# A hybrid attention / delta-net layer on one core: the arena moved to a multiple of 1,024 bytes, weight tiles and constant matrices moved directly behind it

## The chip, the cores and the metric

The kernel runs on one core of a Trainium2 chip. A core has five engines that run on their own and wait for each other through semaphores: TensorE (PE, matrix multiplies, with a separate weight load, PEld, before each), VectorE (DVE), ScalarE (ACT), GpSimd (POOL) and SyncE (SP), whose queue issues all the loads and stores here. Operands lie in the on-chip memory SBUF, as 128 partitions; a tile is a stretch of bytes at the same offset in each partition. TensorE's results go to PSUM, here one tensor "banks" of eight banks of 512 float32 columns.

The metric is the time of one execution on the device in microseconds (us), the median of several. Lower is better.

## The reference

One layer over 512 latent tokens and 256 context tokens, width 1,024, everything in float32. Cut to what matters:

```python
h  = rms_norm(x, g_norm1) * (1.0 + sc1) + sh1
hc = rms_norm(ctx, g_norm1) * (1.0 + csc1) + csh1
aq, ak, av, dq, dk, dv, dz, da, db, ga, gd = split_cols(h @ w_in)        # the same of hc
y_attn = window_ctx_attention(q_a, k_a, v_a, k_ac, v_ac, attn_sink)
o_dc, s_cf, s_cb = bidir_delta(*dn_inputs(cdq, cdk, cdv, cda, cdb), s_zero, s_zero)
o_dl, _, _ = bidir_delta(*dn_inputs(dq, dk, dv, da, db), s_cf, s_cb)
y = jax.nn.sigmoid(ga) * (y_attn @ w_br_attn) + jax.nn.sigmoid(gd) * (y_d @ w_br_dn)
x_new = x + gt1 * (y @ w_out)
hm = rms_norm(x_new, g_norm2) * (1.0 + sc2) + sh2
out = x_new + gt2 * (jnp.square(jax.nn.relu(hm @ w_mlp1)) @ w_mlp2)       # hidden width 4,096
```

`y_d` is the delta-net output, normalised and gated with `silu(dz)`. The shifts, scales and gates `sh, sc, gt` come from `silu(c) @ w_ada + b_ada`.

## The kernel before, in words

**Layout of the work.** Activations are kept transposed: 128 features by tokens, so that a weight tile of 128 x 128 is TensorE's weight operand and the activations stream past it, 512 or 256 columns (tokens) in one matmul. Each float32 operand is split in two parts, a rounded one (hi) and the rest (lo), and each product of two tiles is made of three matmuls into the same bank: hi by hi, hi by lo, lo by hi. That is `mm3` with L299 (`w[0]`, `xhi`), L300 (`w[0]`, `xlo`) and L301 (`w[1]`, `xhi`); L978 (gate tiles), L1024 (attention branch) and L1427 (`Pair.prod`) write out the same three.

**Where things lie in SBUF.** Two kinds of memory hold nearly all operands:

- The **arena** is one tensor of 167 units of 1,024 bytes per partition, allocated first (L107 and L108). `mem` hands out stretches of whole units; the tensors called `m` in the profile are such stretches. Activations, their hi and lo parts, and in some places weights lie there.
- **Pools** behind it: `const` holds constants (`ones`, `ident`, `bones`, `identb`, `maskb`, `prm` and small per-token tables), `sb` holds the rotating **weight tiles** of 4,096 bytes that `wload` (L243 to L252) uses: `wr`, the raw weights as loaded, four buffers; `wh` and `wl`, hi and lo, two buffers each. A weight tile holds eight 128 x 128 pieces of 512 bytes.

The pools are laid out one behind the other in the order in which they are opened, and within `const` each tile is put at the next multiple of 32 bytes. Worked out from the program, in bytes from the start of a partition:

| tensor | starts at | past a multiple of 1,024 by |
|---|---|---|
| arena (so every `m`) | 16,512 | 128 |
| `ones` | 188,352 | 960 |
| `ident` | 189,184 | 768 |
| `wr`, four tiles | 194,912 and on | 352 |
| `wh`, two tiles | 211,296 and on | 352 |
| `wl`, two tiles | 219,488 and on | 352 |

The 352 is 32 bytes past a multiple of 64; the offset comes from small constants of 4 bytes, `nega` (L636) the last of them.

**Stages** (times as in the trace). Up to about 48 us the modulation weights and the inputs are loaded and three tiles of the input projection are begun while they arrive; those three have their `wh` and `wl` in the arena. Up to about 480 us the input projection's tiles (512 latent columns alone, or in turn 512 and 256 with the context), the attention and the delta-net run woven into each other; the code weaves them by counts (`weave`, `QTS`, `FILL`, `INV`). From about 480 us on TensorE works through gate tiles, the branch and output projections, and the MLP: the output projection's last three tiles run in two halves of 256 columns (L1356, about 554 to 573 us), the first MLP group of 8 hidden tiles multiplies a moving operand of two pieces of 256 columns with weights in the arena (L1514, about 585 to 625 us), and the other three groups form each pair of hidden tiles from **seven** products of 256-column blocks in place of eight (`Pair`, L1427, weights and activations both in the arena). The second MLP product of all four groups reads `wh` and `wl` (from L1542 on).

**Order of the work.** The tile framework inserts the semaphores; each engine runs its instructions in program order. Loads are issued by SP in program order, a `wr` buffer's next load when ACT (L250) and DVE (L251) have read it.

Of the kernel before, what the change touches and what calls it, by code (L numbers as in the profile page):

```python
# [8 lines left out]
F32 = mybir.dt.float32  # L9
F32R = mybir.dt.float32r  # L10
BF16 = mybir.dt.bfloat16
# [5 lines left out]
NU = 167  # L17
NWR, NWS = 4, 2
# [16 lines left out]
P = 128  # L35
D = 1024
KT = D // P
# [65 lines left out]
def tile_layer(ctx: ExitStack, tc: tile.TileContext, I: dict, out: bass.AP, dbg=None):  # L103
    nc = tc.nc
    V, A, G, PE = nc.vector, nc.scalar, nc.gpsimd, nc.tensor

    base = -(-nc._sbuf_addr_for_side("left") // 32) * 32  # L107
    nc.alloc_sbuf_tensor("arena", [P, NU * 256], F32, side="left")  # L108
    const = ctx.enter_context(tc.tile_pool(name="const", bufs=1))
    sb = ctx.enter_context(tc.tile_pool(name="sb", bufs=1))  # L110
    ps = ctx.enter_context(tc.tile_pool(name="ps", bufs=1, space=PSUM))
# [2 lines left out]
    def nm(s):  # L114
        uid[0] += 1
        return f"{s}_{uid[0]}"
# [7 lines left out]

    alloc, bank = mem.get, lambda n=1: banks.get(n * 512)

    def cload(key, shape, dt=F32):
        t = const.tile(list(shape), F32, name=f"c_{key}")
        nc.sync.dma_start(out=t, in_=I[key])
        return t  # L130

# [11 lines left out]
    def act(out_, in_, func, **kw):  # L143

        sets = TABLES.get(func)
        if sets and actg["set"] not in sets:
            head = A.preload_act_table_set(sets[0])
            for o in actg["ops"]:
                tc.add_manual_dep(head.ins, o.name, nosync, reason="table sets")
            actg.update(set=sets[0], head=head.ins, ops=[head.ins])  # L150
        r = A.activation(out_, in_, func, **kw)  # L151
        if sets:
            tc.add_manual_dep(r.ins, actg["head"].name, nosync, reason="table sets")
            actg["ops"].append(r.ins)
        return r


    cc = cload("cc", [P, KT, 2])
    prm = cload("prm", [P, 188])
    ones = const.tile([P, P], F32, name="ones")  # L160
    V.memset(ones, 1.0)
    epsc = const.tile([P, 1], F32, name="epsc")
    V.memset(epsc, EPS)
# [77 lines left out]
        mp_.free()  # L241

    def wload(src, n=KT, bufs=None):  # L243
        raw = sb.tile([P, KT, P], F32, tag="wr", bufs=NWR, name=nm("wr"))[:, :n]
        nc.sync.dma_start(out=raw, in_=src)
        if bufs:
            hi, lo = (b.ap.rearrange("p (k c) -> p k c", k=KT) for b in bufs)
        else:
            hi, lo = (sb.tile([P, KT, P], F32, tag=t, bufs=NWS, name=nm(t))[:, :n] for t in ("wh", "wl"))
        A.activation(r32(hi), raw, AF.Copy)  # L250
        V.tensor_tensor(r32(lo), raw, hi, op=ALU.subtract)  # L251
        return r32(hi), r32(lo)  # L252
# [4 lines left out]
    def load_early():  # L257
        bb = alloc(1024), alloc(1024)
        ebufs.extend(bb)
        early.append((wload(I["win"][list(EARLY)[len(early)]], bufs=bb), bank(2)))  # L260
# [53 lines left out]
    for kt in range(KT):  # L314
        t = alloc(768)
# [15 lines left out]
        b.free()  # L331


    ident = cload("ident", [P, P])
    bones = cload("bones", [P, P])
    identb = const.tile([P, P], BF16, name="identb")
    V.tensor_copy(identb, ident)
    maskb = const.tile([P, 2, P], BF16, name="maskb")
    mt = alloc(256)
    nc.sync.dma_start(out=mt.ap, in_=I["masks"])  # L340
    V.tensor_copy(maskb, mt.ap.rearrange("p (d k) -> p d k", d=2))
# [20 lines left out]
    wq += [(I["wbr"][0, ct], 4) for ct in range(8)] + [(I["win"][t + i], KT) for t, i in gates[ND1:]]  # L362
    wq += [(I["wbr"][1, ct], 4) for ct in range(8)] + [(I["wout"][ct], KT) for ct in range(8)]
    wq = [lambda a=a: wload(*a) for a in wq]
    wn = [wq.pop(0)()]

# [266 lines left out]
            V.scalar_tensor_tensor(y, y, scale, t.ap, op0=ALU.mult, op1=ALU.mult)  # L633
        t.free()

    nega = const.tile([16, 1], F32, name="nega")  # L636
    act(nega, alog[0:16], AF.Exp)
    V.tensor_scalar(nega, nega, -1.0, None, op0=ALU.mult)

# [5 lines left out]
    t, t2 = alloc(TOK), alloc(TOK)  # L645
# [392 lines left out]
    def late_mod(grp):  # L1038

        for j in range(8):  # L1040
            wa = sb.tile([P, KT, P], F32, tag="wr", bufs=NWR, name=nm("wa")).rearrange("p k c -> p (k c)")
            nc.sync.dma_start(out=wa, in_=I["wada2"][grp, j])
            t = alloc(1024)
            V.scalar_tensor_tensor(t.ap, wa, 0.5, scr.ap, op0=ALU.mult, op1=ALU.mult, accum_out=modT[:, grp, j:j + 1])  # L1044
            t.free()
            if j == 7:
                V.tensor_tensor(modT[:, grp], modT[:, grp], bada[:, 16 + 8 * grp:24 + 8 * grp], op=ALU.add)
            yield

    late = (x for grp in range(4) for x in late_mod(grp))  # L1050
    late_n = [0]

# [141 lines left out]
    for g in range(2):  # L1194
        ms = slice(16 * g, 16 * g + 16)
        f, b = xa[0][:, ms], xa[1][:, ms]
# [8 lines left out]
    for g in range(2):  # L1205
# [12 lines left out]
        for a in range(2):  # L1218
            lo, hi = quad(a, 0), quad(a, 1)
# [36 lines left out]
    for qq in range(2):  # L1256
# [3 lines left out]
        for a in range(2):  # L1260
            n = 2 * qq + a
            t = alloc(512)
# [86 lines left out]
    def load_first():  # L1349
        for i in range(NHALF):  # L1350
            bufs = [alloc(1024), alloc(1024)]
            first.append([bufs, wload(I["wm1"][i], bufs=bufs)])
# [152 lines left out]
    for hf in range(4):  # L1505
        act_, xs = [], []
        for f in range(0 if hf else FT):
            if first:
                bufs, _, acc = first.pop(0)
            else:  # L1510
                bufs = [alloc(1024), alloc(1024)]
# [162 lines left out]
```

## Time and profile before

| | |
|---|---|
| time, median of 3 runs | 932.66 us (932.61 to 935.09) |
| the profiled execution | 930.84 us, its span 929.1 us |
| TensorE (PE) busy | 903.2 us, 97% of the span, 8,228 matmuls |
| weight loads (PEld) busy | 747.0 us, 80% |
| VectorE busy | 665.0 us, 72% |
| ScalarE busy | 482.7 us, 52% |
| moved by DMA | 98.79 MB, 106 GB/s in the mean |
| TensorE's granted clock | full all through |

A matmul's row shows a start and a duration. Matmuls are pipelined: a row's duration (about 0.39 us for 512 columns) is longer than the distance to the next start. In this document the **pitch** is that distance, from one matmul's start to the next one's. A row of `wh` or `wl` among the inputs says that the weights came from a rotating weight tile; `banks<-m,m` says that both operands came from the arena. "fp32r" marks operands that are streamed in the rounded form; the profile's shapes of matmuls say f32 for all.

### The profile page before, as it was taken

What the parts mean: (1) busy time and instruction counts of PE and PEld (TensorE: products, weight loads), DVE (VectorE), ACT (ScalarE), POOL (GpSimd) and SP (SyncE); (2) the same over time, 40 slices, a digit from 0 to 9 for tenths busy, and PEclk for the clock granted to TensorE, in tenths of its full rate; (3) what the DMA queues carried; (4) which work ended last, traced back from release to release, by engine and by line L of the source; (5) the groups of instructions that cost most, each with busy time, mean ns of one, the idle gap of its engine ahead of it and who ended that gap; (6) DMA issues with size and microseconds to landing.
All of it is one profiled execution on the core that took longest, in us unless ns stands there. A gap on an engine that the chain in (4) does not pass through costs nothing.

```text
span 929.1 us, 19276 instructions
## 1 busy us (share of the span) xinstructions
PE 903.2 (97%) x8228; PEld 747.0 (80%) x8228; DVE 665.0 (72%) x1116; ACT 482.7 (52%) x857; POOL 12.0 (1%) x26
## 2 busy tenths in 40 slices
PE   9999999988999999999999999999999999999998
PEld 7688677867777787778888788988898899889976
DVE  4666799996777997367865978995587377637632
ACT  5467654356567787475554434563355146415520
POOL 0000000000000002000000000000000000000000
PEclk9999999999999999999999999999999999999999
DMA  9911111110000232324524575543413340233021
GB/s 356 369 48 46 48 48 68 52 42 23 24 13 23 58 115 78 108 86 146 173 80 147 170 258 196 182 136 113 136 47 105 100 159 29 89 114 120 14 91 45
DMA packets 29605, 98.79 MB, mean 106 GB/s; under 512 B 3664, under 2 KB 4176, under 8 KB 29520
## 3 DMA queue, kind: packets, MB, share of 16 engines
q1 hardware_dynamic: 29520, 97.57, 30.7%
q8 instruction: 64, 1.05, 0.5%
q14 instruction: 21, 0.17, 0.1%
HBM read 95.46 MB, written 2.10 MB: 105 GB/s over the span
## 4 chain that ended last, share of the span: by engine, by line
PE 72%; DVE 15%; ACT 6%; DMA 4%; issue 2%; ACTq 0%; DVEq 0%
PE banks L299 12%; PE banks L300 12%; PE banks L301 12%; PE banks L1427 11%; PE banks L978 10%; DVE wl L251 2%; PE banks L1024 2%; PE banks L1090 2%; ACT m L151 2%; DMA wa<-in_wada 1%; DMA m<-in_wm 1%; DVE m L188 1%; PE banks L193 1%; PE banks L563 1%; PE banks L1121 1%
## 5 line engine op out<-in xcount | busy, mean ns | idle before, releaser
L299 PE MATMUL banks<-m,wh 128*128 128x512 f32 (+1 forms) x568 | 214.6, 379 | 0.5 <-ACT wh L250 0.2
L301 PE MATMUL banks<-m,wl 128*128 128x512 f32 (+1 forms) x568 | 212.5, 376 | 2.1 <-DVE wl L251 2.1
L300 PE MATMUL banks<-m,wh 128*128 128x512 f32 (+1 forms) x568 | 212.1, 374 | 0.0
L250 ACT ACTIVATE wh<-wr 128x1024 fp32r<-128x1024 f32 (+1 forms) x92 | 90.4, 984 | 139.1 <-PE banks L300 115.7
L251 DVE TENSOR_TENSOR wl<-wr,wh 128x1024 fp32r<-128x1024 f32 (+1 forms) x92 | 103.7, 1128 | 34.2 <-ACT wh L250 31.7
L1427 PE MATMUL banks<-m,m 128*128 128x256 f32 x1008 | 124.0, 284 | 1.5 <-DMA m<-in_wm 0.7
L301 PEld LDWEIGHTS banks<-m,wl 128*128 128x128 f32 x568 | 106.2, 188 | 23.6 <-DVE wl L251 3.5
L1427 PEld LDWEIGHTS banks<-m,m 128*128 128x128 f32 x1008 | 122.2, 192 | 3.5 <-DVE m L188 1.2
L299 PEld LDWEIGHTS banks<-m,wh 128*128 128x128 f32 x568 | 106.6, 188 | 22.5 <-ACT wh L250 0.9
L300 PEld LDWEIGHTS banks<-m,wh 128*128 128x128 f32 x568 | 106.7, 188 | 19.8 <-issue 0.2
L187 ACT ACTIVATE m<-m 128x512 fp32r<-128x512 f32 (+2 forms) x118 | 82.3, 720 | 76.2 <-DVE m L1285 12.8
L188 DVE TENSOR_TENSOR m<-m,m 128x512 fp32r<-128x512 f32 (+2 forms) x118 | 92.4, 804 | 22.0 <-ACT m L187 17.0
L978 PE MATMUL banks<-m,wh 128*128 128x512 f32 x320 | 105.0, 402 | 1.3 <-ACT m L151 1.1
L1554 DVE SCALAR_TENSOR_TENSOR m<-banks,modT,m 128x512 f32<-128x512 f32 x32 | 24.0, 749 | 85.7 <-PE banks L301 85.7
L978 PEld LDWEIGHTS banks<-m,wh 128*128 128x128 f32 x320 | 59.2, 188 | 14.4 <-ACT m L151 1.3
L978 PE MATMUL banks<-m,wl 128*128 128x512 f32 x160 | 65.7, 410 | 0.0
L299 PE MATMUL banks<-m,m 128*128 128x256 f32 (+1 forms) x136 | 44.5, 342 | 2.0 <-ACT m L305 1.2
L1044 DVE SCALAR_TENSOR_TENSOR m<-wa,m 128x1024 f32<-128x1024 f32 x32 | 38.9, 1219 | 10.4 <-DMA wa<-in_wada 10.3
L300 PE MATMUL banks<-m,m 128*128 128x256 f32 (+1 forms) x136 | 45.4, 341 | 0.0
L301 PE MATMUL banks<-m,m 128*128 128x256 f32 (+1 forms) x136 | 44.5, 336 | 0.1
L151 ACT ACTIVATE m<-banks,st 128x512 f32<-128x512 f32 (+1 forms) x32 | 23.5, 739 | 25.8 <-DVE st L520 25.7
L978 PEld LDWEIGHTS banks<-m,wl 128*128 128x128 f32 x160 | 30.0, 188 | 7.0
(254 smaller groups left out, 1352.6 us busy)
## 6 DMA issues: line engine op xcount, KB each, us to landing
wr<-in_wm SPq DMA_DIRECT2D x40, 512.0 KB, 3.8
wr<-in_win SPq DMA_DIRECT2D x39, 512.0 KB, 3.3
wa<-in_wada SPq DMA_DIRECT2D x32, 512.0 KB, 3.6
m<-in_wm SPq DMA_DIRECT2D x24, 512.0 KB, 3.3
m<-in_wada SPq DMA_DIRECT2D x16, 512.0 KB, 10.2
m<-in_xT SPq DMA_DIRECT2D x8, 512.0 KB, 5.2
wr<-in_wbr SPq DMA_DIRECT2D x16, 256.0 KB, 2.7
wr<-in_wout SPq DMA_DIRECT2D x8, 512.0 KB, 4.3
```

The lines of the kernel that those rows point to most:

```text
L151: r = A.activation(out_, in_, func, **kw)
L187: A.activation(r32(hi), src, AF.Copy)
L188: (eng or V).tensor_tensor(r32(lo), src, hi, op=ALU.subtract)
L250: A.activation(r32(hi), raw, AF.Copy)
L251: V.tensor_tensor(r32(lo), raw, hi, op=ALU.subtract)
L299: PE.matmul(acc, w[0][:, k, :], xhi, start=(start and i == 0), stop=False)
L300: PE.matmul(acc, w[0][:, k, :], xlo, start=False, stop=False)
L301: PE.matmul(acc, w[1][:, k, :], xhi, start=False, stop=(stop and i == n - 1))
L978: PE.matmul(acc.ap, w[x][:, k, :], hx[k][y], start=(k == p == 0), stop=(k == KT - 1 and p == 2))
L1044: V.scalar_tensor_tensor(t.ap, wa, 0.5, scr.ap, op0=ALU.mult, op1=ALU.mult, accum_out=modT[:, grp, j:j + 1])
L1427: PE.matmul(dst, r32(self.w[w][i][:, k * P:(k + 1) * P]), xs7[x][k][j], start=(n == 0), stop=(n == 11))
L1554: V.scalar_tensor_tensor(xn_[ct], accs[ct].ap, modT[:, 3, ct:ct + 1], xn_[ct], op0=ALU.mult, op1=ALU.add)
```

## The change

The arena starts at the next multiple of 1,024 bytes. Two pools are opened directly behind it: `wp` with the weight tiles `wr`, `wh`, `wl`, and `mats` with the constant matrices `ones`, `ident`, `bones`, `identb`, `maskb`. The small constants follow. `nega` is made 64 bytes long and its first column is used, so that what stands behind it starts at a multiple of 64.

```diff
-    base = -(-nc._sbuf_addr_for_side("left") // 32) * 32
-    nc.alloc_sbuf_tensor("arena", [P, NU * 256], F32, side="left")
+    low = -(-nc._sbuf_addr_for_side("left") // 32) * 32
+    base = -(-low // 1024) * 1024
+    nc.alloc_sbuf_tensor("arena", [P, NU * 256 + (base - low) // 4], F32, side="left")
+    wp = ctx.enter_context(tc.tile_pool(name="wp", bufs=1))
+    mats = ctx.enter_context(tc.tile_pool(name="mats", bufs=1))
     const = ctx.enter_context(tc.tile_pool(name="const", bufs=1))
     sb = ctx.enter_context(tc.tile_pool(name="sb", bufs=1))
...
-    def cload(key, shape, dt=F32):
-        t = const.tile(list(shape), F32, name=f"c_{key}")
+    def cload(key, shape, pool=const):
+        t = pool.tile(list(shape), F32, name=f"c_{key}")
...
-    ones = const.tile([P, P], F32, name="ones")
+    ones = mats.tile([P, P], F32, name="ones")
...
-        raw = sb.tile([P, KT, P], F32, tag="wr", bufs=NWR, name=nm("wr"))[:, :n]
+        raw = wp.tile([P, KT, P], F32, tag="wr", bufs=NWR, name=nm("wr"))[:, :n]
...
-            hi, lo = (sb.tile([P, KT, P], F32, tag=t, bufs=NWS, name=nm(t))[:, :n] for t in ("wh", "wl"))
+            hi, lo = (wp.tile([P, KT, P], F32, tag=t, bufs=NWS, name=nm(t))[:, :n] for t in ("wh", "wl"))
...
-    ident = cload("ident", [P, P])
-    bones = cload("bones", [P, P])
-    identb = const.tile([P, P], BF16, name="identb")
+    ident = cload("ident", [P, P], mats)
+    bones = cload("bones", [P, P], mats)
+    identb = mats.tile([P, P], BF16, name="identb")
...
-    maskb = const.tile([P, 2, P], BF16, name="maskb")
+    maskb = mats.tile([P, 2, P], BF16, name="maskb")
...
-    nega = const.tile([16, 1], F32, name="nega")
+    nega = const.tile([16, 16], F32, name="nega")[:, :1]
...
-            wa = sb.tile([P, KT, P], F32, tag="wr", bufs=NWR, name=nm("wa")).rearrange("p k c -> p (k c)")
+            wa = wp.tile([P, KT, P], F32, tag="wr", bufs=NWR, name=nm("wa")).rearrange("p k c -> p (k c)")
```

Where the tensors lie after it, again from the program:

| tensor | starts at | past a multiple of 1,024 by |
|---|---|---|
| arena (so every `m`) | 17,408 | 0 |
| `wr`, four tiles | 188,416 and on | 0 |
| `wh`, two tiles | 204,800 and on | 0 |
| `wl`, two tiles | 212,992 and on | 0 |
| `ones` | 221,184 | 0 |
| `ident` | 221,696 | 512 |

Every arena tensor moves by 896 bytes, every weight tile by -6,496 bytes. The instructions are the same ones: on each of the five engines they stand in the same order, with the same shapes and the same waits, and differ in their addresses alone (and in the row length of `nega`).

## The prediction

> **What bounds the kernel now.** I read the page first, then the busy time by stage, then what TensorE (PE) waits for, and last the rows of its matmuls in order of time. From the page:
>
> ```profile
> span 929.1 us, 19276 instructions
> PE 903.2 (97%) x8228; PEld 747.0 (80%) x8228; DVE 665.0 (72%) x1116; ACT 482.7 (52%) x857; POOL 12.0 (1%) x26
> ...
> PE 72%; DVE 15%; ACT 6%; DMA 4%; issue 2%; ACTq 0%; DVEq 0%
> ```
>
> PE is busy for 97% of the span and holds 72% of the chain that ended last. The windows' columns are the stretch, its length, the busy time of PE, PEld, DVE, ACT and POOL, PE's granted clock (1.00 is full), the DMA share and GB/s:
>
> ```profile
> 50.00:475.00 425.00, 409.57 (x5305) 325.80 (x5298) 334.25 (x608) 265.90 (x551) 11.83 (x22) 1.00 0.21 68
> 475.00:930.00 455.00, 446.56 (x2590) 386.66 (x2588) 301.97 (x448) 192.22 (x269) 0.00 (x0) 1.00 0.34 116
> ```
>
> From 475 us on PE lacks 8.4 us of full, at the full clock. No cause keeps it waiting for more than 1.2 us in all there; the two longest:
>
> ```profile
> PE banks L299 <- ACT m L305: 1.2, 1, 1.2
> PE banks L301 <- DVE wl L251: 0.7, 3, 0.3
> ```
>
> So in the second half, time is the number of matmuls by their pitch. What a new address can change is the pitch. It is worth reading row by row: the first number is the start. A run with weights from `wh` and `wl`, 512 columns, first and last of 24 rows:
>
> ```profile
> 705.65 0.39 PE L299 MATMUL banks<-m,wh 128*128 128x512 f32 x1
> ...
> 711.02 0.40 PE L301 MATMUL banks<-m,wl 128*128 128x512 f32 x1
> ```
>
> 23 steps in 5.37 us: 233.5 ns. A run of 512 columns with weights from the arena, first and last of 19 rows:
>
> ```profile
> 594.32 0.39 PE L301 MATMUL banks<-m,m 128*128 128x512 f32 x1
> ...
> 598.40 0.39 PE L301 MATMUL banks<-m,m 128*128 128x512 f32 x1
> ```
>
> 18 steps in 4.08 us: 226.7 ns. The clock, the shape and the neighbours on the other engines are alike; 6.7 ns (3%) lie between them. With 256 columns it is the other way round: `wh`/`wl` first (72 rows), then the seven-product blocks from the arena:
>
> ```profile
> 554.58 0.28 PE L299 MATMUL banks<-m,wh 128*128 128x256 f32 x1
> ...
> 562.86 0.28 PE L301 MATMUL banks<-m,wl 128*128 128x256 f32 x1
> ```
>
> ```profile
> 699.43 6.38 PE L1427 MATMUL banks<-m,m 128*128 128x256 f32 x52
> 705.65 0.39 PE L299 MATMUL banks<-m,wh 128*128 128x512 f32 x1
> ```
>
> 71 steps in 8.28 us are 116.6 ns; 52 steps from 699.43 to 705.65 are 119.6 ns. The pattern that I read in this: with weight tiles the pitch is in proportion to the columns (233.5 is twice 116.6); with both operands in the arena it is 106.5 ns per 256 columns plus the same 13 ns for each matmul, long or short. Before the change, arena weights and arena activations start at the same place within each 512 bytes (both at 128), while a weight tile starts at 352. That is the one thing which the change makes equal for weight tiles too.
>
> **The change part by part.** No instruction, load or wait is added, removed or moved, so no queue changes.
>
> *DVE and ACT.* The split of a weight tile (L250, L251) now reads and writes at other addresses. The groups by form hold DVE's part at both alignments already:
>
> ```profile
> L251 DVE TENSOR_TENSOR wl<-wr,wh 128x1024 fp32r<-128x1024 f32 x76 | 92.8, 1221 | 28.4 <-ACT wh L250 25.9
> L188 DVE TENSOR_TENSOR m<-m,m 128x1024 fp32r<-128x1024 f32 x26 | 31.8, 1222 | 8.1 <-ACT m L187 7.9
> ```
>
> 1,221 ns with all three operands in weight tiles against 1,222 with all in the arena: the 352 and the 128 make no difference there. Zero, and from 475 us on DVE and ACT are busy for 302 and 192 of 455 us, so some ns on either would lie beside PE's work.
>
> *Weight tiles, 512 columns, from 475 us on.* The groups of this stretch (the L301 group stands for three alike, L299, L300 and L301):
>
> ```profile
> L301 PE MATMUL banks<-m,wl 128*128 128x512 f32 x328 | 129.8, 396 | 0.5 <-DVE wl L251 0.5
> ...
> L1427 PE MATMUL banks<-m,m 128*128 128x256 f32 x1008 | 124.0, 284 | 1.5 <-DMA m<-in_wm 0.7 <-DVE m L188 0.5
> L978 PE MATMUL banks<-m,wh 128*128 128x512 f32 x70 | 22.3, 397 | 0.0
> ...
> L978 PE MATMUL banks<-m,wl 128*128 128x512 f32 x36 | 14.5, 403 | 0.0
> ...
> L301 PE MATMUL banks<-m,wl 128*128 128x256 f32 x48 | 13.3, 281 | 0.2 <-DVE wl L251 0.2
> ```
>
> 3 x 328 + 70 + 36 = 1,090 matmuls. From 233.5 to 226.7 ns they save 1,090 x 6.8 = 7.4 us. The arena run at 594 us differs from them in a second way: its moving operand is two pieces of 256 columns. So I looked for whole 512-column pieces with arena weights next to weight tiles:
>
> ```profile
> 101.49 0.39 PE L753 MATMUL banks<-m,m 128*128 128x512 f32 x1
> ...
> 102.40 0.39 PE L299 MATMUL banks<-m,wh 128*128 128x512 f32 x1
> ...
> 103.10 0.39 PE L753 MATMUL banks<-m,m 128*128 128x512 f32 x1
> ```
>
> Four from the arena (L753, L754) take 0.91 us, 227.5 each; the next three, from weight tiles, 0.70, 233.3 each. That speaks for the weights' place and against the two pieces. Bounds: no gain (0), and 13.5 ns each if 512 columns came down to 0.22 us, twice the shortest step between rows of 256 columns in the 554 us run (0.11): 14.7 us. I take the middle one, the 7.4 that two rows show.
>
> *Weight tiles, 256 columns, from 475 us on.* 3 x 48 = 144 matmuls that would go from 116.6 to 119.6: +0.4 us.
>
> *The same between 50 and 475 us.* The two largest groups there:
>
> ```profile
> L978 PE MATMUL banks<-m,wh 128*128 128x512 f32 x250 | 82.6, 403 | 1.3 <-ACT m L151 1.1 <-DVE m L578 0.2
> L299 PE MATMUL banks<-m,wh 128*128 128x512 f32 x128 | 53.2, 416 | 0.3 <-ACT wh L250 0.2
> ```
>
> With the `wl` half of L978's and the L300 and L301 beside each L299 that is 250 + 125 + 3 x 128 = 759 with 512 columns: 5.2 us at 6.8 ns. Little of it is in long runs, DVE is on the chain there, and runs that alternate 512 and 256 don't show the arena's gain:
>
> ```profile
> 52.38 0.40 PE L299 MATMUL banks<-m,m 128*128 128x512 f32 x1
> ...
> 59.73 0.40 PE L299 MATMUL banks<-m,m 128*128 128x512 f32 x1
> ```
>
> 42 rows, seven rounds of three by 512 and three by 256, in 7.35 us: 1.05 us a round, which is 3 x 233.5 + 3 x 116.6, though all weights lie in the arena. I count a quarter, 1.3 us; bounds 0 and 5.2.
>
> *The seven-product blocks and the arena's own start.* L1427 keeps both operands in one arena, so they keep their places relative to each other; only the start goes from 128 past 1,024 to 0. No row shows an operand of such a run that starts there. I take 0; one more or one less step of 6.7 ns for each of 1,008 matmuls is 6.8 us either way.
>
> *DMA.* In the first two of 40 slices, 46 us, DMA is full:
>
> ```profile
> DMA  9911111110000232324524575543413340233021
> ```
>
> Every tile that is filled there starts off a multiple of 256 bytes before and on one after. Nothing in the trace prices that; 0. The Trainium skill, DMA: Bandwidth & Descriptors, "How a descriptor splits into AXI transactions", says that a descriptor which starts off a 256-byte boundary pays for the bytes before it. For 4,096 bytes at 128 past that would be 132 beats in place of 128, by my estimate from that page 3% of the full stretch or 1.4 us less; no run here shows it yet, and it would take the sum to -9.7.
>
> **Sum.** -7.4 + 0.4 - 1.3 = -8.3 us. The profiled execution of 930.84 us (span 929.1) would take 922.5. The median of the runs shown, 932.66, is 1.8 us above that execution, so I forecast 924.4.
>
> **The rivals.**
>
> *A: nothing moves.* The round at 52 us has arena weights and still the slow pitch, so the fast one may come from something else than the weights' place, such as the two pieces. Then the long runs stay at 233.5: 932.7. Against it: the four rows at 101 us, and the 116.6 against 119.6 for 256 columns. A rule says the same as this rival: the Trainium skill, TensorE: Matmul & The Clock Gate, "Step-by-step: what each phase is for", has two independent read ports, so that loading the next weights takes nothing from the running matmul; by it the place of the weights could not matter. The pitches of this trace that differ with the weights' place speak against it.
>
> *B: the start at 1,024 counts by itself.* If the 13 ns per matmul are paid for pieces that begin inside a block, they shrink for the arena as well: the 1,090 at 13.5 ns (14.7 us), L1427 from 119.6 to 113 (6.7 us), the 144 from 116.6 to 113 (0.5 us), and a quarter of the 759 at 13.5 ns (2.6 us): -24.5 us, 908.2. For it: proportional pitches can't come from one weight load per matmul alone. Against it: no row shows a pitch below 0.11 or 0.22 us.
>
> *C: slower.* With every operand on the same start, the weight load and the moving operand of each block meet at the same place always. The 256-column runs already pay 3 ns more in the arena than in weight tiles. If exact alignment costs L1427 and the 144 (1,152 in all) one more step of 6.7 ns while 512 columns stay as they are: +7.7 us, 940.4. It decides once L1427's pitch is above 122.5 ns, from where it costs more than the 2.8 us that can be told. For it: alignment made the 256-column pitch worse, not better. Against it: their relative places don't change.
>
> **How the numbers follow.** A change under 0.3% (2.8 us) can't be told from none: the three runs alone spread by 2.5 us. The forecast, with sizes from half to one and a half of it (920 to 928.5), has a chance of 0.40; B 0.20; A 0.22; C 0.18. Faster: 0.60, the same 0.22, slower 0.18. B and C are shapes with unsure sizes; the range takes in all of A, half of B's spread down to 908 and half of C's up to 940, which leaves out about 0.2.
>
> **What would show it.** Right: in the second half the pitch of L299 to L301 with `wh` and `wl` is about 227 ns, that of the 256-column run at 554 us about 120, L1427's stays at 120, DVE and ACT means stay within 5 ns, and nearly all of the gain comes after 475 us. Wrong: a pitch still at 233 (A), L1427 well under 120 (B) or above 122.5 (C). It would be wrong in another way if PE got faster and then waited, for `wl` (L251) or for the weights of the MLP, where the longest of its waits add up to 1.2 and 0.7 us now.

## The result: 0.5% faster, and the profile after

The changed kernel takes 928.99 us (median of 15 executions, 926.39 to 932.51). The kernel before, measured beside it, takes 934.0 us (15 executions, 931.9 to 936.6). The ratio is 0.9948, with a 95% interval from 0.9934 to 0.9961: 5.0 us less. The forecast was 924.4, a step of -8.3 us. The direction and the mechanism held, but some 40% of the step did not reach the end. The profiled execution of the changed kernel took 928.46 us (before: 930.84, quicker than all 15 timed ones). Two executions further below, of 1,090.22 and 1,443.82 us, ran at a granted clock of 0.75 and 0.56 in the mean and are left out of the medians there.

From the page of the changed kernel: the span, the busy time of the engines, and the chain that ended last.

```profile
span 926.7 us, 19276 instructions
PE 897.7 (97%) x8228; PEld 748.8 (81%) x8228; DVE 665.5 (72%) x1116; ACT 482.4 (52%) x857; POOL 12.1 (1%) x26
...
PE 64%; DVE 19%; ACT 7%; DMA 6%; issue 3%; SPq 0%; DVEq 0%; ACTq 0%
```

PE is busy for 5.5 us less, with the same 8,228 matmuls. The span fell by 2.4 us, so the idle time rose from 25.9 to 29.0 us. PE's share of the chain went from 72% to 64%, and DVE's, ACT's and DMA's shares rose. These are the signs of a bound engine that got faster and now waits for others.

The rows of PE in order of time that answer to those of the prediction. 512 columns from weight tiles, first and last of 24 rows; then 256 columns from weight tiles, first and last of 43 rows (the lines of the changed file are 3 higher, so L299 is L302):

```profile
703.58 0.40 PE L302 MATMUL banks<-m,wh 128*128 128x512 f32 x1
...
708.82 0.39 PE L304 MATMUL banks<-m,wl 128*128 128x512 f32 x1
```

```profile
555.78 0.28 PE L302 MATMUL banks<-m,wh 128*128 128x256 f32 x1
...
560.82 0.28 PE L302 MATMUL banks<-m,wh 128*128 128x256 f32 x1
```

23 steps in 5.24 us are 227.8 ns, where there were 233.5. 42 steps in 5.04 us are 120.0 ns, where there were 116.6. The same two pitches, as means over all regular steps (start to start, without those that hold a wait) from 470 us on:

| from 470 us on | before | after |
|---|---|---|
| 512 columns, weight tiles | 233.33 ns (1,070 steps) | 227.07 ns (1,065 steps) |
| 256 columns, weight tiles | 116.69 ns (134) | 119.5 ns (some 130) |
| 256 columns, both operands in the arena (L1427, now L1430) | 119.80 ns (1,115) | 119.8 ns (some 1,100) |
| 512 columns in two pieces, both in the arena | 226.95 ns (118) | 226.95 ns (119) |

DVE's groups by form did not move: 1,222 ns after for 1,221 before, and 1,223 for 1,222.

```profile
L254 DVE TENSOR_TENSOR wl<-wr,wh 128x1024 fp32r<-128x1024 f32 x76 | 92.9, 1222 | 28.0 <-ACT wh L253 25.6
...
L191 DVE TENSOR_TENSOR m<-m,m 128x1024 fp32r<-128x1024 f32 x26 | 31.8, 1223 | 8.1 <-ACT m L190 7.9
```

What did change is what PE waits for from 475 us on. Before, the two longest sums were 1.2 and 0.7 us. After:

```profile
PE banks L304 <- DVE wl L254: 2.1, 4, 1.1
PE banks L1430 <- DMA m<-in_wm: 2.0, 1, 2.0
PE banks L302 <- ACT m L308: 1.2, 1, 1.2
PE banks L1430 <- DVE m L191: 0.8, 2, 0.6
PE banks L1430 <- DVE m L1407: 0.3, 1, 0.3
```

**A ledger.** Both kernels issue the same matmuls in the same order, so the start of each can be compared with its own start before. The columns split the difference (after minus before, us, one profiled execution each) into regular steps with 512 columns from weight tiles, those with 256, and all the rest, which are mostly steps that hold a wait. The last two columns are a second profile of the changed kernel (the control run below) against the same profile of before. As that profile is an unusually quick execution, the sums, -2.3 and -3.0 us, come out smaller than the 5.0 us between the medians.

| stretch (us, before) | 512 columns, weight tiles | 256 columns, weight tiles | rest | sum | second profile: rest | sum |
|---|---|---|---|---|---|---|
| 0 to 50 | | | +0.09 | +0.09 | +0.53 | +0.53 |
| 50 to 475 | -1.41 | 0.00 | -0.41 | -1.82 | +1.26 | -0.21 |
| 475 to 545 | -1.55 | | +0.15 | -1.40 | +0.15 | -1.41 |
| 545 to 577 | -0.26 | +0.45 | +1.12 | +1.31 | +1.57 | +1.76 |
| 577 to 684 | -1.24 | | +0.99 | -0.25 | +0.81 | -0.43 |
| 684 to 849 | -2.23 | | +0.22 | -2.01 | +0.28 | -1.93 |
| 849 to 875 | | | +2.87 | +2.87 | -0.18 | -0.18 |
| 875 to the end | -1.16 | | +0.05 | -1.11 | +0.05 | -1.11 |
| all | -7.85 | +0.45 | +5.08 | -2.32 | +4.47 | -2.98 |

The pitch brought 7.4 us (7.85 less 0.45), nearly all that the prediction counted on. Between 50 and 475 us it brought little, and the rows show why: 512-column steps with a 256-column matmul within four places did not move (232.6 ns before, 232.4 after, 196 steps), while those among 512-column matmuls alone went from 233.2 to 228.3 ns (201 steps). The rest took part of the gain back. Two losses appear in both profiles: 1.1 to 1.6 us between 545 and 577 us, and 0.8 to 1.0 between 577 and 684. One large loss, 2.87 us near 856 us, appears only in the first. It is a wait of 2.0 us for a load of MLP weights, and right behind it PE's granted clock is halved for 3.41 us (windows: the stretch, its length, the busy time of PE, PEld, DVE, ACT and POOL, the granted clock, DMA share and GB/s):

```profile
856.00:858.00 2.00, 0.94 (x8) 0.73 (x7) 1.29 (x2) 1.88 (x4) 0.00 (x0) 1.00 0.18 64
858.00:860.00 2.00, 1.08 (x8) 1.08 (x9) 1.10 (x2) 0.89 (x1) 0.00 (x0) 0.93 0.01 4
860.00:862.00 2.00, 2.00 (x11) 2.00 (x11) 2.00 (x4) 1.77 (x2) 0.00 (x0) 0.50 0.00 0
862.00:864.00 2.00, 2.00 (x15) 2.00 (x14) 1.74 (x3) 1.29 (x4) 0.00 (x0) 0.72 0.00 0
```

Of the 2.87 us, 1.49 lie in regular steps at the lower clock and 1.38 in the wait.

### The profile page after: what moved, and what is told of

Its sections match the earlier page's. It is cut to its first block, busy times and chain, and to the rows that moved or that the text cites. A ratio compares the mean times of both kernels' runs of the same rounds, so it can differ in the third digit from the quotient of the medians.

```text
span 926.7 us, 19276 instructions
## 1 busy us (share of the span) xinstructions
PE 897.7 (97%) x8228; PEld 748.8 (81%) x8228; DVE 665.5 (72%) x1116; ACT 482.4 (52%) x857; POOL 12.1 (1%) x26
## 4 chain that ended last, share of the span: by engine, by line
PE 64%; DVE 19%; ACT 7%; DMA 6%; issue 3%; SPq 0%; DVEq 0%; ACTq 0%
PE banks L1430 11%; PE banks L302 10%; PE banks L303 10%; PE banks L304 10%; PE banks L981 9%; DVE wl L254 3%; DVE m L191 2%; DMA m<-in_wm 2%; PE banks L1027 2%; PE banks L1093 2%; DMA wa<-in_wada 2%; ACT m L154 1%; DVE m L811 1%; PE banks L566 1%; DVE m L810 1%
## 5 line engine op out<-in xcount | busy, mean ns | idle before, releaser
L304 PE MATMUL banks<-m,wl 128*128 128x512 f32 (+1 forms) x568 | 210.6, 373 | 3.5 <-DVE wl L254 3.5
L302 PE MATMUL banks<-m,wh 128*128 128x512 f32 (+1 forms) x568 | 213.0, 376 | 0.6 <-ACT wh L253 0.2
L303 PE MATMUL banks<-m,wh 128*128 128x512 f32 (+1 forms) x568 | 210.3, 370 | 0.0
L1430 PE MATMUL banks<-m,m 128*128 128x256 f32 x1008 | 125.7, 286 | 3.3 <-DMA m<-in_wm 2.0
L1430 PEld LDWEIGHTS banks<-m,m 128*128 128x128 f32 x1008 | 123.8, 194 | 5.5 <-DMA m<-in_wm 2.2
L304 PEld LDWEIGHTS banks<-m,wl 128*128 128x128 f32 x568 | 106.5, 188 | 23.3 <-DVE wl L254 5.4
L302 PEld LDWEIGHTS banks<-m,wh 128*128 128x128 f32 x568 | 107.0, 188 | 20.0 <-ACT wh L253 1.3
L303 PEld LDWEIGHTS banks<-m,wh 128*128 128x128 f32 x568 | 107.0, 188 | 17.7 <-DVE m L191 0.3
L302 PE MATMUL banks<-m,m 128*128 128x256 f32 (+1 forms) x136 | 44.7, 342 | 2.0 <-ACT m L308 1.2
L1047 DVE SCALAR_TENSOR_TENSOR m<-wa,m 128x1024 f32<-128x1024 f32 x32 | 39.0, 1220 | 9.9 <-DMA wa<-in_wada 9.7
L303 PE MATMUL banks<-m,m 128*128 128x256 f32 (+1 forms) x136 | 45.4, 341 | 0.0
L304 PE MATMUL banks<-m,m 128*128 128x256 f32 (+1 forms) x136 | 44.5, 337 | 0.1
```

The lines of the kernel that those rows point to most:

```text
L302: PE.matmul(acc, w[0][:, k, :], xhi, start=(start and i == 0), stop=False)
L303: PE.matmul(acc, w[0][:, k, :], xlo, start=False, stop=False)
L304: PE.matmul(acc, w[1][:, k, :], xhi, start=False, stop=(stop and i == n - 1))
L1430: PE.matmul(dst, r32(self.w[w][i][:, k * P:(k + 1) * P]), xs7[x][k][j], start=(n == 0), stop=(n == 11))
```

## The experiments

Three questions were open. What about the new addresses sets the pitch? Does the same rule hold for the seven-product blocks? Where did the lost part go? Each edit is against the changed kernel unless it says otherwise.

### What sets the pitch: the relative place, or the absolute one

The first four kernels differ from the changed one in two numbers only: where the arena starts within 1,024 bytes, and how many bytes lie between the arena's end and the weight tiles (W). The arena's length is a multiple of 1,024, so W is also the weights' place relative to the moving operand. The edit, with `A` and `W` filled in:

```
-    base = -(-low // 1024) * 1024
-    nc.alloc_sbuf_tensor("arena", [P, NU * 256 + (base - low) // 4], F32, side="left")
+    base = low // 1024 * 1024 + A
+    nc.alloc_sbuf_tensor("arena", [P, NU * 256 + (base - low + W) // 4], F32, side="left")
```

Where the arena starts at 128 the file has one line more, so L303 to L305 are L302 to L304 of the changed kernel.

With the arena at 0 (the line for `base` stays as it is) and W = 224, the relative place of before:

> The changed kernel with its arena at a multiple of 1,024 bytes, but weight tiles and constant matrices 224 bytes further: a weight tile then stands to an arena tile as in the kernel before (352 against 128). Theory P (the place of the weights against the moving operand counts): the long runs of 512 columns with wh and wl go back to 233 ns, the 256-column run of the output projection to 116.7, seven-product blocks stay at 120; time about 4 to 8 us above the changed kernel. Theory K (the arena's start at a multiple of 1,024 counts): 227 ns stays. Theory S (a weight tile must start at a multiple of 64 bytes; 224 is 32 past one): 233 ns as with P.

With the arena at 128, its place before the change, and W = 0:

> The changed kernel with the arena 128 bytes past a multiple of 1,024, where it was before, and weight tiles directly behind it, so at 128 too. P: 227 ns in the long 512-column runs with wh and wl, 119 to 120 in the 256-column run, as in the changed kernel. S: the same. K: 233 ns and 116.7, as before.

With the arena at 128 and W = 256:

> Arena at 128, weight tiles 256 bytes further at 384: both at multiples of 64 bytes, but half of 512 bytes apart. P with a period of 512 bytes: 233 ns and 116.7. P with a period of 256 bytes or less, and S: 227 ns and 120.

With the arena at 0 and W = 64:

> Arena at a multiple of 1,024, weight tiles 64 bytes further. S: 227 ns and 120, as in the changed kernel. P: another pitch, 233 ns and 116.7 if the lock needs equal places; if the pitch depends on the place in steps, any value between 220 and 240 for 512 columns.

Two more with the arena at 0 map the places in between, W = 32 and W = 128:

> As the changed kernel, but the weight tiles start 32 bytes past a multiple of 1,024; arena at a multiple of 1,024. So weights minus moving operand is 32. At 0 a 512-column step with weight tiles took 227.1 ns, at 64 it took 233.4. Theory P64 (the place counts in blocks of 64 bytes): 32 lies in the block of 0, so 227.1 for 512 columns and 119.5 for 256, about 929.3 us. Theory P32 (it counts finer, only 0 is fast): 233.4 for 512 columns, 256 columns under 119.5, about 933 us.

> As the changed kernel, but the weight tiles start 128 bytes past a multiple of 1,024. Weights minus moving operand is 128. Theory with a period of 256 bytes: 128 is not 0, so 512 columns take 233.4 ns and 256 columns 115 to 117, about 933 us. Theory with a period of 128 bytes: 128 is as good as 0, 227.1 and 119.5, about 929.3 us.

What was measured (means of the regular steps from 470 us on; the time of the one profiled execution each; beside the first four tests the kernel before took 933.92 us in one execution, beside the last two 933.65 in the median of 19):

| kernel | arena mod 1,024 | weights minus moving, mod 256 | 512 columns, weight tiles | 256 columns, weight tiles | blocks in the arena | us |
|---|---|---|---|---|---|---|
| before | 128 | 224 | 233.33 | 116.69 | 119.80 | 930.84 |
| after | 0 | 0 | 227.07 | 119.51 | 119.8 | 928.46 |
| W = 224 | 0 | 224 | 233.32 | 116.76 | 119.86 | 937.72 |
| both at 128 | 128 | 0 | 227.14 | 119.50 | 119.84 | 929.30 |
| W = 256 | 128 | 0 | 227.18 | 119.47 | 119.83 | 929.41 |
| W = 64 | 0 | 64 | 233.38 | 115.07 | 119.85 | 932.77 |
| W = 32 | 0 | 32 | 233.27 | 118.17 | 119.78 | 935.51 |
| W = 128 | 0 | 128 | 232.66 | 119.31 | 119.75 | 932.37 |

A single time carries the pauses and the clock of its execution (W = 224 has pauses of 1.5 and 2.1 us behind 545 us and stretches of half clock near 25 and 571 us); these runs are read by their pitch. The rows that decide, PE in order of time, 24 rows of 512 columns each. W = 256 with the arena at 128:

```profile
705.36 0.40 PE L303 MATMUL banks<-m,wh 128*128 128x512 f32 x1
...
710.60 0.39 PE L305 MATMUL banks<-m,wl 128*128 128x512 f32 x1
```

W = 64, a multiple of 64 but not the place of the moving operand, with 24 rows of 512 columns and then 31 rows of 256:

```profile
707.96 0.40 PE L302 MATMUL banks<-m,wh 128*128 128x512 f32 x1
...
713.33 0.40 PE L304 MATMUL banks<-m,wl 128*128 128x512 f32 x1
```

```profile
559.54 0.28 PE L304 MATMUL banks<-m,wl 128*128 128x256 f32 x1
...
562.94 0.28 PE L304 MATMUL banks<-m,wl 128*128 128x256 f32 x1
```

W = 128, again 24 rows of 512 columns:

```profile
706.03 0.39 PE L302 MATMUL banks<-m,wh 128*128 128x512 f32 x1
...
711.37 0.39 PE L304 MATMUL banks<-m,wl 128*128 128x512 f32 x1
```

23 steps take 5.24 us (227.8 ns each) at W = 256, 5.37 (233.5) at W = 64 and 5.34 (232.2) at W = 128. What follows:

- **The arena's start at a multiple of 1,024 does nothing by itself.** With the old relative place on the new start the old pitch is back (233.32), and with the new relative place on the old start the new pitch stays (227.14). That was the condition of the prediction's rival B, which falls.
- **A start at a multiple of 64 is not enough** (W = 64: 233.38).
- **The place counts with a period of 256 bytes, not 128.** 256 is as good as 0. 32, 64, 128 and 224 are all slow for 512 columns. (The next section adds a second pair: -192, which is 64 by this period, gives the 256-column pitch of 64.)
- **For 256 columns the order is another.** 64 is the best place: 30 steps from 559.54 to 562.94 us take 3.40 us, 113.3 ns each, half of the fast pitch for 512 columns (the mean of all such steps at 64 is 115.07). 0 and 128 are the worst of those tried.

### The seven-product blocks at the better place

The blocks of L1430 are 1,008 matmuls with 256 columns and both operands in the arena, so at place 0. Four of the seven products read their moving operand from `AS`. These were shifted by 48 columns (192 bytes, so weights minus moving is 64), which needs blocks of nine arena units in place of eight; the twin has the same blocks without the shift (`0:2048`). The edit, with its factors of 1 worked out:

```
-        AS = [alloc(2048, True) for _ in range(4)]
+        big = [alloc(2048 + 256, True) for _ in range(4)]
+        AS = [big[n][:, 48:48 + 2048] for n in range(4)]
```

> As the changed kernel, but the moving operands of four of the seven products in the 256-column blocks (S1 to S4) lie 48 columns (192 bytes) further on in blocks of 9 arena units in place of 8, so that weights minus moving is 64 by a period of 256 bytes; the other three products and all 512-column work keep 0. Theory (the relative place sets the step, whichever buffers they are): the 576 matmuls of these products go from 119.8 to 115.1 ns, the other 432 stay at 119.8, 2.7 us less than its twin without the 48 columns. Rival (arena operands of these blocks have their step for another reason): all 1,008 stay at 119.8 and the times of the two are equal.

> The twin of the kernel with the 48 columns: the same blocks of 9 units, same order of work and waits on all engines, but the operands start at the blocks' start, so the relative place is 0 everywhere. Both theories expect 119.8 ns for all 1,008 matmuls of the blocks. Its time against the changed kernel (929.0 us) tells what the other buffers and the other order of work alone do; no theory here puts a number on that.

In the shifted kernel the matmuls of these products (556 regular steps) have a pitch of 115.0 ns, and the others keep 119.2. In the twin all have 119.7. So the rule is one of addresses, whichever of the two operands is moved and whichever buffers they are in. A row of 122 matmuls in each, PE in order of time (at the end of a row stands the wait ahead of it), first the shifted kernel and then the twin:

```profile
671.44 15.09 PE L1430 MATMUL banks<-m,m 128*128 128x256 f32 x122 [1.51 <-DVE m L191]
```

```profile
670.57 15.45 PE L1430 MATMUL banks<-m,m 128*128 128x256 f32 x122 [1.00 <-DVE m L191]
```

0.36 us less over 122 matmuls is 3.0 ns each. The time did not follow. The shifted kernel takes 936.93 us (10 executions, 933.38 to 942.36; ratio to the kernel before 1.0037, 1.0014 to 1.0060) and the twin 936.48 (9 executions, 931.55 to 937.51; ratio 1.0024, 1.0004 to 1.0044). The expectation of 2.7 us between them failed. In the rows above, the wait for DVE's split of the weights is longer (1.51 for 1.00 us) by more than the row is shorter. Over all of the stretch from 475 us on, PE's listed waits add up to 13.0 us in the shifted kernel's profile and 11.9 in the twin's, and the first has two stretches of half clock there that the second has not. One profile of each doesn't separate what the faster pitch caused from the chance of an execution; that the gain was not seen is what is measured. The other buffers, with the order of work that they bring, cost some 7 us (a ratio of 1.0024 to the kernel before, where the changed kernel has 0.9948); why was not taken apart.

### Where the lost part went

Between 545 and 577 us the out projection's last column tiles run in halves. Their weights go through the same four raw buffers as the tiles of the late modulation (L1047, 13 of them from 473 to 572 us), and DVE splits the one and sums the other. The test issues three of the late tiles per column tile in place of two, so that more of them lie before 545 us:

```
-        run_late(2)
+        run_late(3)
```

> The changed kernel with three late modulation tiles per column tile of the output projection in place of two, so that more of these loads (which share the four raw buffers with the weights) and their VectorE work come before 545 us and fewer between 545 and 575. Theory G1 (of the 3.1 us that TensorE is ahead at 545 us, 1.3 are lost because the split weights of the last column tiles wait behind these loads and sums): the waits for the split weights between 550 and 565 us (1 to 2 us in the changed kernel) go, and the time falls by about 1.3 us, 927.7. Rival (the end of that stretch is set by the chain of sums and the norm, whatever is loaded): the waits stay or move to 475 to 545 us, and the time stays at 929 or rises by up to 2 us.

The changed kernel once more, on the same chip, as the control:

> The changed kernel once more, as the control on the chip of the next two runs. All theories: 929 us, a ratio of 0.995 to the kernel before, 512-column steps with weight tiles at 227.1 ns, and a wait of 0.5 to 2.5 us of a seven-product block for a load of MLP weights near 856 us.

The control takes 927.36 us (8 executions, 925.58 to 931.45; ratio to the kernel before, 932.9 us, 0.9944, 0.9924 to 0.9964). With three late tiles it is 926.22 us (6 executions, 923.73 to 928.17; 0.9931, 0.9906 to 0.9956). The waits of PE from 545 to 577 us, first the control, then three late tiles:

```profile
PE banks L304 <- DVE wl L254: 1.3, 1, 1.3
PE banks L302 <- ACT m L308: 1.2, 1, 1.2
PE banks L302 <- DVE m L1308: 0.2, 1, 0.2
```

```profile
PE banks L302 <- ACT m L308: 1.2, 1, 1.2
PE banks L304 <- DVE wl L254: 0.2, 1, 0.2
```

The wait for the split weights is gone, and by the ledger the stretch moves by -0.32 us against before, where the control moves by +1.76: 2.1 us come back. The medians differ by 1.1 us; their intervals overlap, so the whole time alone would not show it.

The same edit on the kernel before tells whether the late tiles are a gain by themselves:

> The kernel before (old addresses, 233.3 ns for 512-column steps with weight tiles), with the same three late modulation tiles per column tile of the output projection in place of two. Theory G1 (the loads and sums between 545 and 575 us bound that stretch only once TensorE runs ahead of them): the kernel before had waits of some 0.2 us for split weights there, so it gains 0 to 0.7 us, 932.2 to 932.9 beside 932.9. Rival (the earlier tiles are a gain by themselves, with any address): it gains the 1.1 to 2 us that they brought with the new addresses, 931 to 931.8.

It takes 931.9 us (13 executions, 930.8 to 936.47) beside 932.84; the ratio is 0.9986, 0.9972 to 1.0001. That lies between the two expectations and settles nothing. The stretch does: from 545 to 577 us the edit moves the kernel before by +0.32 us. There the waits of PE with the edit are these, and the profile without it has the first and the last of them alone, so there was nothing to win:

```profile
PE banks L299 <- ACT m L305: 1.2, 1, 1.2
PE banks L299 <- DVE m L1305: 0.4, 1, 0.4
PE banks L301 <- DVE wl L251: 0.2, 1, 0.2
```

What the wait hangs on can be read in the first profile of the changed kernel, from its views of DVE, SP, ACT and PE, put in order of time:

```profile
545.62 1.22 DVE L1047 SCALAR_TENSOR_TENSOR m<-wa,m 128x1024 f32<-128x1024 f32 x1
546.88 0.33 SPq L248 DMA_DIRECT2D wr<-in_wm  x1
551.40 1.06 ACT L253 ACTIVATE m<-wr 128x1024 fp32r<-128x1024 f32 x1 [2.82 <-DMA wr<-in_wm]
552.49 1.22 DVE L254 TENSOR_TENSOR m<-wr,m 128x1024 fp32r<-128x1024 f32 x1 [2.84 <-ACT m L253]
554.29 1.22 DVE L254 TENSOR_TENSOR wl<-wr,wh 128x1024 fp32r<-128x1024 f32 x1
555.56 0.39 PE L304 MATMUL banks<-m,wl 128*128 128x256 f32 x1 [1.11 <-DVE wl L254]
```

A late tile's sum ends at 546.84 us and frees a raw buffer; the load of the first MLP tile into that buffer is issued at 546.88 and lands 4.5 us later; ACT and DVE split this tile first, by program order, and only then comes the `wl` that PE needs. In the kernel before, the same split was done at 557.41 us and PE needed it at 557.61: it had 0.20 us of room. At 545 us PE had gained 3.1 us in the first profile, while this sum had gained only 2.0 (545.62 after, 547.66 before). PE ran ahead of the work that feeds it by more than the room, and waited. With three late tiles an output projection tile's split, not a sum, stands ahead of that load: it is issued at 546.9 us, where the control has 549.2.

The other profiles agree as far as this one wait goes. At this matmul the six with the fast pitch and two late tiles wait 1.1 (after), 1.3 (the control), 0.9 (both at 128), 1.6 (W = 256), 0.9 (shifted) and 0.2 us (twin); none of the six with the old pitch (before, with three late tiles, W = 224, 64, 32 and 128) waits there. The loss of the whole stretch is not the fast pitch's alone, though. From 545 to 577 us, W = 224 and W = 32 lose 3.5 and 3.9 us against the same profile of before with the old pitch: they wait 1.5 and 1.9 us for a later `wl`, behind a late tile's load that took 6.3 and 6.4 us, and half clock follows. W = 64 loses 0.8 there, W = 128 0.1. So the ledger's 1.1 to 1.6 us, measured against one quick profile, are not the price of the fast pitch in every execution.

The last test concerns the load near 856 us. The second pair's loads of a stage were issued after the seventh column tile of the stage before, in place of after the eighth:

```
+            if hf < 3 and ct == 6:
+                pairs[hf + 1][1].fetch()
```

`fetch` issues the two loads with which `load1` begins; the rest of `load1` stays where it was.

> The changed kernel, in which the loads of the second pair of MLP weights of a stage are issued after the seventh of eight column tiles of the stage before, in place of after the eighth; the arithmetic on them stays where it is. Theory G2 (the load that lands at 858 us is late, and the pause is followed by 3.4 us of half clock): the wait for the load near 856 us goes, and 0.6 to 2.3 us of wait and up to 1.7 us of clock come back, about 927. Rival (other buffers are reused then and another product waits in its place): the waits of the seven-product blocks add up to as much as before, 929 or more.

It takes 928.89 us (7 executions, 926.17 to 929.22; ratio 0.9953, 0.9936 to 0.9970) beside the control's 927.36: no gain. Its profiled execution is the one of 1,443.82 us, so where the other executions wait can't be read, and whether another wait took the place of this one stays open. The other profiles show that this loss is not the change's. The control, with the same program, waits 0.2 us for that load. The kernel before with three late tiles, on the old addresses, waits 2.4 us for it, and its clock is then halved as well:

```profile
863.00:866.00 3.00, 0.62 (x6) 0.42 (x5) 1.01 (x3) 2.19 (x3) 0.00 (x0) 1.00 0.05 15
866.00:868.00 2.00, 2.00 (x12) 2.00 (x12) 2.00 (x4) 0.95 (x1) 0.00 (x0) 0.52 0.00 0
868.00:870.00 2.00, 2.00 (x13) 2.00 (x13) 1.74 (x3) 1.57 (x3) 0.00 (x0) 0.63 0.00 0
```

Over the profiles with this order of work the wait is 0.2, 0.3, 0.4, 2.0 and 2.3 us with the fast pitch, and 0.3, 0.4, 0.7, 1.8, 2.1 and 2.4 with the old one. That it cost the first profile 2.87 us is the luck of that execution.

## Why the prediction was right, step by step

**What bounds the kernel.** Right: in the second half the time is the number of matmuls by their pitch, until the pitch falls. That "no cause keeps it waiting for more than 1.2 us in all there" was true of that profile only. The pattern of 13 ns for each matmul is no fixed cost: at place 64, 233.38 and 115.07 ns would make it negative (115.07 less the 118.31 between them).

**DVE and ACT: 0.** Right; 1,222 and 1,223 ns after.

**Weight tiles, 512 columns, from 475 us on: -7.4.** The mechanism was right and the size nearly so. The pitch fell by 6.26 ns (233.33 to 227.07), not 6.8: the prediction read 6.8 off two runs of 24 and 19 rows. The ledger has -6.4 us over the steps that it can compare.

**Weight tiles, 256 columns: +0.4.** Right, +0.45.

**The woven part, a quarter of 5.2, -1.3.** The size held: -1.41 and -1.49 in the two profiles. Yet other steps of that stretch moved by -0.41 in one profile and +1.26 in the other, so of this term nothing reliable reaches 475 us. The reason for taking a quarter held: steps next to 256-column matmuls did not gain.

**The seven-product blocks and the arena's own start: 0.** Right; 119.8 before and after, and the four kernels with the arena at 0 and 128 show that its start alone does nothing.

**DMA: 0.** Right. The two opening slices read 362 and 366 GB/s where before they had 356 and 369, and the matmuls of the opening start 0.09 us later at 50 us, not earlier. The GB/s of 40 slices, before and after:

```profile
GB/s 356 369 48 46 48 48 68 52 42 23 24 13 23 58 115 78 108 86 146 173 80 147 170 258 196 182 136 113 136 47 105 100 159 29 89 114 120 14 91 45
```

```profile
GB/s 362 366 47 47 48 48 69 47 46 24 22 15 23 58 115 72 115 93 140 182 71 148 184 252 190 179 140 113 137 47 109 103 152 43 94 129 99 2 91 45
```

The estimate of 1.4 us that stood beside this term, from the Trainium skill, DMA: Bandwidth & Descriptors, "How a descriptor splits into AXI transactions", is not borne out for these loads.

**The sum: where it failed.** The sum let all of the pitch's gain through to the end; it had no term for what PE meets when it is early. The text named this as the way to go wrong ("if PE got faster and then waited, for `wl` (L251) or for the weights of the MLP"), and it gave it no price. (Of the 1.2 and 0.7 us that it names, the rows put 0.7 on `wl`; the 1.2 is a wait for ACT's L305.) The trace of before held the size of the room at the first place: 0.20 us. The pitch brought 7.4 us. At that `wl` the fast pitch waits 0.2 to 1.6 us, and the test with three late tiles shows the cause. By the ledger, the stretch from 545 to 577 us took 1.1 to 1.6 us and the one from 577 to 684, where both profiles hold steps with longer waits than before, 0.8 to 1.0 (0.2 and 0.8 in the kernels with both at 128 and W = 256); the cause of the second was not tested. Together that is 2.1 and 2.4 us in the two profiles, which would make 7.4 into the 5.0 to 5.5 that the medians of the two comparisons show. That sum is an account that fits, not one that is shown: it rests on one quick profile of before, and old-pitch kernels lose as much in the same stretch in some executions. How the lost part divides over the stretches stays open. The second place, the MLP weights, gave back nothing that can be put down to the change. The absolute number missed by 4.6 us for a second reason too: the kernel before took 934.0 us this time, not 932.66. So 928.99 lies just above the forecast's own band of 920 to 928.5, while the step of 5.0 us lies within half to one and a half of 8.3.

**The rivals.** A (nothing moves) fell with the first row of 227 ns. The rule beside it, two independent read ports in the Trainium skill, TensorE: Matmul & The Clock Gate, "Step-by-step: what each phase is for", does not agree with these runs: with the same program and the same clock, the weights' place alone moves the 512-column step between 227.1 and 233.4 ns. B fell with the arena at 128 and the same pitch. C fell: L1430 stays at 119.8, far from 122.5.

## What to carry to other kernels

When fp32r matmuls with 512 columns run back to back, put the weight tile and the moving operand at the same place within 256 bytes, and look at the pitch of each kind of matmul by itself: here 512 and 256 columns want different places, and where the two alternate the 512-column step did not gain. A gain on the bound engine lasts only until its next feeder; before adding it up, read in each stretch how long before its use each operand is ready (here 0.20 us for a split behind four raw buffers). Compare the same instruction's start in both records, stretch by stretch, and take a second profile of both kernels, the old one too, before explaining a single pause.

## What the hardware showed unexpectedly

- The step of an fp32r matmul depends on the place of its weights relative to its moving operand, with a period of 256 bytes: 227.1 ns at 0 and 232.7 to 233.4 at 32, 64, 128 and 224 for 512 columns; 119.5 at 0, 118.2 at 32, 115.1 (113.3 in the run of 31 rows above) at 64, 119.3 at 128 and 116.7 at 224 for 256 columns. Only these five places were tried. Why the two lengths disagree stays open.
- A pause of PE can cost as much again in clock. From 475 us to shortly before the end, thirteen profiles hold six stretches of half clock, each 3.41 us long. Four began within 1.5 us behind a pause of 1.5 to 2.4 us, and two (in the shifted kernel) behind two or three pauses of 0.7 to 1.2 us close together. Pauses of 1.5 to 2.3 us in seven other places (W = 224 at 866 us, W = 256 at 556 and 859, W = 128 at 861, the shifted kernel at 670 and 894, the twin at 892) had none behind them, so the length of the pause alone does not decide.
